# Splits of weight blocks scheduled 64 instructions ahead of their use, between the first gates and the second, in a two-layer hybrid decoder trunk

## The chip, the cores and the metric

The kernel runs on one core of a Trainium2 chip. A core has a matrix engine (TensorE, PE in the profile), a vector engine (VectorE, DVE), a scalar engine (ScalarE, ACT), a general engine (GpSimd, POOL) and a queue engine (SyncE, SP). Each works through its own list of instructions in order and waits for the others by semaphores. The metric is the device time of one execution in microseconds (us).

## The reference

The input is `x`, 512 tokens of width 1024, all in float32. Each of the two layers does this, cut to what matters here:

```python
h = rmsnorm(x, norm_mix)
z = h @ w_in                       # q_a k_a v_a | q_m k_m v_m o_m | i/f logits | gates A, B
att = sliding_window_attention(q_a, k_a, v_a, sinks)  # 8 heads of 64, 2 kv heads, window 128
hm = mlstm_chunkwise(q_m, k_m, v_m, i_pre, f_pre)     # 4 heads, chunks of 64
hm = rmsnorm(hm, m_head_norm) * sigmoid(o_m)
mixed = sigmoid(g_a) * (att @ w_att_branch) + sigmoid(g_m) * (hm @ w_m_branch)
x = x + mixed @ w_out
u = relu(rmsnorm(x, norm_ffn) @ w_ff1)
x = x + (u * u) @ w_ff2            # width 4096
```

## The kernel before

Each layer is a `mixer` (everything up to `mixed @ w_out`) and then an `mlp`. The 512 tokens stay on the chip. Weights come from memory in blocks of 128 rows by 512 columns, and every product is made from float32 numbers that are split in two parts: `wh` is the rounded high part, `wl` the rest. A product of two split numbers is three matmuls (`mm3`).

The function `chunk` (L139) provides one such block. It loads the block into a tile `w` (pool `wraw`, three buffers) by a DMA that SyncE issues (L155), ScalarE copies it to `wh` (L165), and VectorE subtracts `wh` from `w` to get `wl` (L166). The pool `wsp` holds four pairs `wh`, `wl`. So a load needs the split of three blocks before to be done, and a split needs the products of four blocks before to be done. In `group_steps` four result tiles are built over the blocks: a block serves 4 x 3 matmuls, and after the last block `finish` evicts the four results.

The order of the instructions comes from a scheduler. The program is written as one list, and the scheduler takes, of what is ready in its model, the instruction that comes first in priority, which is its place in the program. Code inside `tc.high_priority()` is treated as if it stood in front of everything. With a number, `tc.high_priority(64)`, it is treated as if it stood that many instructions ahead of its own place. `tc.issue_after` adds an edge to the order. All of `chunk` stands in `tc.high_priority()`.

Work of other kinds is put between the matmul steps by `weave(fill, side)`: `fill` is the list of matmul steps with a width, and `side` a list of functions with places along it. In the mixer's first `weave` (it ends at L416) the attention queries, keys and values and the gate logits are projected. In the second, which ends at L1062, the `fill` is the projection of the mLSTM queries and keys, the first half of the branch gates (`s0`, `s1`), the value and output-gate products (`vo_steps`, `a_steps`) and the second half of the gates (`s2`, `s3`); its `side` holds the attention units and the mLSTM's own work.

The pieces of the attention that the prediction names are these. L561 to L564 turn the keys of one block of tokens into `kT`: ScalarE scales the high parts, VectorE subtracts the low part (L563) and casts it (L564) for the second head. L583 and L584 do the same for the queries. The scores are products `aux<-kT,t`; L603 copies them, L610 to L621 are the softmax, L52 transposes the probabilities, L175 and L176 split them, GpSimd masks them by a select (L636), and `aux<-t,v` multiplies them by the values.

The value and output-gate products are made by a scheme of seven products with sums of weight blocks. These sums are built in tiles `a`: SyncE loads one block (L716), GpSimd adds others by accumulating DMAs (L720, L732), and L725 and L726 split the sum. Two of the seven products take plain blocks through `chunk`. L769, L770 and L777 form sums `sc` of the inputs, L680 and L683 are products of the gating, L475 is a scan over the gate logits and L915 multiplies a gate into its result.

Of the kernel before, what the change touches and what calls it, by code (L numbers as in the profile page):

```python
# [33 lines left out]
def hybrid_kernel(ctx, tc, x, norm_mix, w_in, att_q_norm, att_k_norm, att_sinks, m_gate_bias,  # L34
# [27 lines left out]
    def nm(s):  # L62
        uid[0] += 1
        return f"{s}_{uid[0]}"
# [30 lines left out]
    def sm(shape, tag, bufs=None):  # L95
        return small.tile(list(shape), F32, tag=tag, name=nm(tag), bufs=bufs)

    def f32(ap):
        return ap.bitcast(F32)
# [34 lines left out]
        return gcol[:, 32 + 4 * l + k:33 + 4 * l + k]  # L134


    chunks, asked = [0], [None]

    def chunk(src, width=T):  # L139

        with tc.high_priority():
            raw = now["wraw"].tile([P, T], F32, tag="w", name=nm("w"))
            off = 0
            for s in src:
                n = s.shape[1]
                if first_loads:

                    n0 = {0: 0, 1: 2}.get(chunks[0], len(first_loads) - 1)
                    with tc.issue_after(first_loads[n0].ins):
                        first_weights.append(nc.sync.dma_start(raw[:, off:off + n], s))  # L150
                    chunks[0] += 1
                    if chunks[0] == 8:
                        first_loads.clear()
                else:
                    asked[0] = nc.sync.dma_start(raw[:, off:off + n], s)  # L155
                off += n
            wh = now["wsp"].tile([P, T], F32R, tag="wh", name=nm("wh"))
            wl = now["wsp"].tile([P, T], F32R, tag="wl", name=nm("wl"))
            n = chunks[0] - 1 if first_loads else 2
            with ExitStack() as order:  # L160
                if n < 1:

                    order.enter_context(tc.issue_after(norm0.hi[n].ins))
                    order.enter_context(tc.issue_after(norm0.lo[n].ins))
                sc.activation(wh[:, :off], raw[:, :off], AF.Copy)  # L165
                ve.tensor_tensor(wl[:, :off], raw[:, :off], f32(wh[:, :off]), op=ALU.subtract)  # L166
        return wh, wl
# [20 lines left out]
    def group_steps(acts, srcs, evac, width, mm, order=None):  # L188


        order = order or list(range(len(acts)))
        ps, w = [], []

        def step(k, m):
            if k == order[0]:
                ps.append(bank())
            if m == 0:
                w[:] = chunk(srcs(k))
            mm(ps[m], slice(m * P, (m + 1) * P), w, acts[k], k == order[0], k == order[-1])

        def finish():
            with tc.high_priority():
                for m in range(4):
                    evac(m, ps[m][:, :width])

        return [(0.25, lambda k=k, m=m: step(k, m)) for k in order for m in range(4)] + [(0, finish)]

    def feat_steps(acts, srcs, evac):

        def mm(ps, c, w, a, first, last):  # L210
            mm3(ps, w[0][:, c], w[1][:, c], a[0], a[1], first, last)

        return group_steps(acts, srcs, evac, T, mm)
# [8 lines left out]
    def weave(fill, side=()):  # L222

        side = sorted(side, key=lambda e: e[0])
        at = 0.0
        for width, f in fill:
            while side and side[0][0] <= at + 1e-6:
                side.pop(0)[1]()
            f()
            at += width  # L230
        for _, f in side:
            f()
# [155 lines left out]
    def mixer(l, norm, late, order, phase):  # L388
# [9 lines left out]
        def wcols(c0, n):  # L398
            return lambda k: [W[k * P:(k + 1) * P, c0:c0 + n]]
# [16 lines left out]
              late + [(6.9, norm.columns), (11.0, lambda: row.append(norm.along()))])  # L416


        ig = sm([P, NB, MH], "ig", 1)
        fg = sm([P, NB, MH], "fg", 1)  # L420
        fa = sm([P, NB, MH], "fa", 1)
# [390 lines left out]
        def vo_step(n, k, i):  # L812
            which, at, outs = plan[n]
            fresh = n in (5, 1, 2, 4) and k == 0
            if fresh and i == 0:
                held[which] = [bank(), bank()]
            if i == 0:
                ready[k] = weight(n, k)
            wh, wl = ready[k]
            if at:  # L820
                c = slice(H * at[0] + i * P, H * at[0] + (i + 1) * P)
                ah, al = (a[:, c] for a in acts[4 * at[1] + k])
            else:
                ah, al = (a[:, k % 2, i * P:(i + 1) * P] for a in sums[n][k // 2])
            mm3(held[which][i], ah, al, wh, wl, fresh, False, skip_group_check=True)
            if k == 3:
                with tc.high_priority():
                    for f, t, first in outs:
                        f(t, i, held[which][i], first)

        def vo_steps(*ns):
            return [(0.25, lambda n=n, k=k, i=i: vo_step(n, k, i))
                    for n in ns for k, i in (by_tokens if n in (6, 7) else by_weights)]
# [78 lines left out]
        def a_steps(g, sg):  # L912
            def ev_a(m, ps):
                t = sg[m]
                ve.scalar_tensor_tensor(t, t, 1.0, ps, op0=ALU.add, op1=ALU.mult)  # L915

            return feat_steps(att_acts, lambda k: [w_att_branch[l, k * P:(k + 1) * P, 512 * g:512 * g + 512]],
                              ev_a)
# [115 lines left out]
        def ready_w(n, k):  # L1034
# [16 lines left out]
            if n == 3:  # L1051
# [8 lines left out]
        side += [(59.6 + 0.75 * k, lambda k=k: ready_w(1, k)) for k in range(3)]  # L1060
        weave(feat_steps(acts, wcols(C_QM, 512), ev_qk) + s0 + s1 + vo_steps(2) + a_steps(0, g0) + a_steps(1, g1)
              + vo_steps(5, 1, 3, 6, 7, 4) + s2 + s3, side)  # L1062

        def m_step(g, m, k):
            if k == 0:
                now_m[g, m] = bank()
            ps, c = now_m[g, m], slice(m * P, (m + 1) * P)
            mm3(ps, *(w[:, c] for w in wm[g, k]), *hmT[k], k == 0, k == 3)
            if k == 3:
                with tc.high_priority():  # L1070
                    merge(g, m, ps)
                    if m % 2:
                        if g:
                            sum1(m // 2)
                        else:
                            direct(0, 0, m // 2)
# [550 lines left out]
    for l in range(DEPTH):  # L1627
        with start if l == 0 else ExitStack() as phase:
            if l > 0:
                psum_pools(phase, 3)  # L1630
            norm = mixer(l, norm, late, order, phase)
        late = norm.steps(0, 1.5, 0.5)
        with ExitStack() as phase:
            psum_pools(phase, 2)
            norm = mlp(l, norm, late, phase)
        late = norm.steps(0, 1.5, 0.5, lambda k, norm=norm: turn_behind(norm, k)) if norm else []
        order = [4, 5, 6, 7, 0, 1, 2, 3]
# [40 lines left out]
```

## Time and profile before

| | |
|---|---|
| time, median of 3 runs | 1290.96 us (1288.26 to 1292.7) |
| profiled execution | 1292.53 us, span 1290.8 us, granted TensorE clock 1.00 |
| TensorE busy | 1273.2 us, 99% of the span |
| VectorE busy | 1043.5 us, 81% |
| ScalarE busy | 795.5 us, 62% |
| GpSimd busy | 265.0 us, 21% |
| memory read | 188.95 MB, 148 GB/s over the span |

The page is one execution. The span is the time from its first instruction to its last; the execution's own time is a little longer. A row of the timeline has the start in us from the start of the span, the busy time in us, the engine, the line, the operation, the tile written and the tiles read, and the count; in brackets stands the idle time ahead of it and who ended it. Layer 1 repeats layer 0 about 640 us later.

### The profile page before, as it was taken

The numbers are of one execution on the slowest core, as the hardware profiler recorded it, in microseconds if no ns is written. First come the engines' busy times: TensorE is split into PE (matmuls) and PEld (weight loads), VectorE is DVE, ScalarE is ACT, GpSimd is POOL, SyncE is SP. The second block draws the span as 40 slices with busy tenths as digits, with TensorE's granted clock in tenths as the row PEclk, the third lists the DMA queues.
The fourth block names the chain that finished last, engine by engine and source line by source line (L and its number), as shares of the span: only waits on it lengthen the run. The fifth ranks groups of instructions, "written<-read, shape, count | busy, mean of one in ns | idle before, by whom it ended". The sixth has DMA issues, their size and how long they took to land.

```text
span 1290.8 us, 19209 instructions
## 1 busy us (share of the span) xinstructions
PE 1273.2 (99%) x6882; PEld 1086.0 (84%) x6882; DVE 1043.5 (81%) x1650; ACT 795.5 (62%) x1403; POOL 265.0 (21%) x341
## 2 busy tenths in 40 slices
PE   9999999999999999999999999999999999999998
PEld 7877778887889999999888777788788899999987
DVE  4688998678687897969948889886887879879697
ACT  5568568645665666656554775785465656665563
POOL 4502142021003021131114022310310030301210
PEclk9999999999999999999999999999999999999999
DMA  5425372576669888898224253734856697988953
GB/s 156 111 75 155 90 131 74 156 129 141 195 164 182 239 181 210 193 210 214 33 75 115 66 148 92 129 99 135 162 136 195 158 212 195 205 213 192 220 142 98
DMA packets 139503, 194.39 MB, mean 151 GB/s; under 512 B 10632, under 2 KB 79088, under 8 KB 139408
## 3 DMA queue, kind: packets, MB, share of 16 engines
q1 hardware_dynamic: 92992, 129.72, 32.8%
q0 software_dynamic: 45696, 63.05, 30.5%
q8 instruction: 54, 0.88, 0.3%
q10 hardware_dynamic: 720, 0.40, 0.1%
q14 instruction: 41, 0.34, 0.1%
HBM read 188.95 MB, written 2.10 MB: 148 GB/s over the span
## 4 chain that ended last, share of the span: by engine, by line
PE 85%; DVE 7%; DMA 3%; ACT 3%; issue 2%; DVEq 0%; SPq 0%; ACTq 0%
PE mm L47 68%; PE aux L47 16%; PE aux L52 2%; DMA qa<-in_w_out_dram 1%; DMA w<-in_w_in_dram 1%; DVE wl L726 1%; DVE wl L166 1%; DVE p L949 1%; DVE a L948 1%; DVE t L176 1%; ACT wh L165 0%; ACT wh L1159 0%; DVE a L698 0%; DVE p L915 0%; DVE m L610 0%
## 5 line engine op out<-in xcount | busy, mean ns | idle before, releaser
L47 PE MATMUL mm<-i,wh 128*128 128x512 f32 (+1 forms) x1280 | 352.8, 362 | 0.3
L1159 ACT ACTIVATE wh<-raw 128x1024 fp32r<-128x1024 f32 x212 | 223.2, 1056 | 177.0 <-PE mm L47 98.6
L1160 DVE TENSOR_TENSOR wl<-raw,wh 128x1024 fp32r<-128x1024 f32 x212 | 255.6, 1220 | 80.2 <-ACT wh L1159 80.1
L47 PEld LDWEIGHTS mm<-i,wh 128*128 128x128 f32 x1280 | 223.0, 189 | 31.1 <-ACT wh L1159 0.7
L47 PE MATMUL mm<-i,wl 128*128 128x512 f32 (+1 forms) x640 | 229.5, 359 | 0.0
L47 PE MATMUL mm<-wh,uh 128*128 128x512 f32 x440 | 171.8, 390 | 0.0
L47 PE MATMUL mm<-wl,uh 128*128 128x512 f32 x440 | 171.7, 390 | 0.0
L47 PE MATMUL mm<-wh,ul 128*128 128x512 f32 x440 | 171.2, 389 | 0.0
L166 DVE TENSOR_TENSOR wl<-w,wh 128x512 fp32r<-128x512 f32 (+1 forms) x144 | 98.7, 689 | 58.1 <-ACT wh L165 56.4
L1329 POOL DMA_DIRECT2D raw<-in_w_ff_dram x48 | 62.6, 1311 | 382.2 <-DMA raw<-in_w_ff_dram 212.2
L47 PEld LDWEIGHTS mm<-i,wl 128*128 128x128 f32 x640 | 121.0, 189 | 17.7
L165 ACT ACTIVATE wh<-w 128x512 fp32r<-128x512 f32 (+1 forms) x144 | 86.7, 604 | 64.3 <-PE mm L47 38.7
L47 PE MATMUL mm<-wh,i 128*128 128x512 f32 (+1 forms) x352 | 101.0, 360 | 2.9 <-ACT wh L165 2.4
L1214 DVE SCALAR_TENSOR_TENSOR x<-mm,ms,x 128x512 f32<-128x512 f32 x126 | 90.5, 744 | 9.1 <-PE mm L47 8.9
L47 PEld LDWEIGHTS mm<-wh,ul 128*128 128x128 f32 x440 | 82.6, 188 | 17.6
L47 PEld LDWEIGHTS mm<-wh,uh 128*128 128x128 f32 x440 | 82.8, 188 | 16.1
L47 PEld LDWEIGHTS mm<-wl,uh 128*128 128x128 f32 x440 | 82.8, 188 | 15.4
L1486 POOL DMA_DIRECT2D raw<-in_w_ff_dram x36 | 43.2, 1200 | 149.3 <-DVE wl L1160 117.2
L47 PEld LDWEIGHTS mm<-wh,i 128*128 128x128 f32 x352 | 62.0, 188 | 13.8 <-ACT wh L165 3.4
L47 PE MATMUL aux<-i,wh 128*128 128x256 f32 x384 | 69.5, 283 | 0.0
L47 PE MATMUL aux<-t,wh 128*128 128x256 f32 x384 | 69.5, 283 | 0.0
L47 PE MATMUL mm<-wl,i 128*128 128x512 f32 (+1 forms) x176 | 62.1, 353 | 0.5 <-DVE wl L166 0.5
(317 smaller groups left out, 2532.7 us busy)
## 6 DMA issues: line engine op xcount, KB each, us to landing
raw<-in_w_ff_dram SPq DMA_DIRECT2D x144, 512.0 KB, 5.1
raw<-in_w_ff_dram POOLq DMA_DIRECT2D x84, 512.0 KB, 7.8
w<-in_w_in_dram SPq DMA_DIRECT2D x112, 256.0 KB, 2.7
a<-in_w_in_dram POOLq DMA_DIRECT2D x32, 256.0 KB, 5.7
qa<-in_w_out_dram POOLq DMA_DIRECT2D x12, 512.0 KB, 6.0
a<-in_w_in_dram SPq DMA_DIRECT2D x16, 256.0 KB, 5.0
w<-in_w_att_branch_dram SPq DMA_DIRECT2D x16, 256.0 KB, 2.7
w<-in_w_m_branch_dram SPq DMA_DIRECT2D x16, 256.0 KB, 2.9
```

What stands on the lines that cost most here:

```text
L47: latest[0] = nc.tensor.matmul(*args, **kw)
L52: latest[0] = nc.tensor.transpose(*args)
L165: sc.activation(wh[:, :off], raw[:, :off], AF.Copy)
L166: ve.tensor_tensor(wl[:, :off], raw[:, :off], f32(wh[:, :off]), op=ALU.subtract)
L176: last_split[1] = ve.tensor_tensor(lo, src, f32(h), op=ALU.subtract)
L726: ve.tensor_tensor(wl, r, f32(wh), op=ALU.subtract)
L948: ve.scalar_tensor_tensor(sgm[g][m], sgm[g][m], 1.0, ps, op0=ALU.add, op1=ALU.mult)
L1159: sc.activation(hi, src, AF.Copy)
L1160: ve.tensor_tensor(lo, src, f32(hi), op=ALU.subtract)
L1214: ve.scalar_tensor_tensor(xh[:, cc], ps[i][:, cc], ms[j][:, b:b + 1], xh[:, cc], op0=ALU.mult, op1=ALU.add)
L1329: gp.dma_start(to[h], src(h, i, j), accum_op=ALU.add)
L1486: gp.dma_start(to[h], src(h, i, j), accum_op=ALU.add)
```

## The change

The split of a block in `chunk` is taken out of the first `tc.high_priority()` and put into a second one, whose argument is `lead[0]`. `None` is the default: in front of everything, as before. In each layer `lead[0]` is 64 from the end of the first `weave` to the end of the second. The load of the block stays as it was.

```diff
-    chunks, asked = [0], [None]
+    chunks, asked, lead = [0], [None], [None]
...
                 else:
                     asked[0] = nc.sync.dma_start(raw[:, off:off + n], s)
                 off += n
+        with tc.high_priority(lead[0]):
             wh = now["wsp"].tile([P, T], F32R, tag="wh", name=nm("wh"))
             wl = now["wsp"].tile([P, T], F32R, tag="wl", name=nm("wl"))
...
               late + [(6.9, norm.columns), (11.0, lambda: row.append(norm.along()))])
 
+        lead[0] = 64
         ig = sm([P, NB, MH], "ig", 1)
...
         weave(feat_steps(acts, wcols(C_QM, 512), ev_qk) + s0 + s1 + vo_steps(2) + a_steps(0, g0) + a_steps(1, g1)
               + vo_steps(5, 1, 3, 6, 7, 4) + s2 + s3, side)
+        lead[0] = None
```

Behind the first added line, the kernel's lines move by 1, behind the second by 2 and behind the third by 3. No engine has an instruction more or less.

**The attention, on VectorE.** Around the cast that completes `kT` for the last block of tokens in layer 0 (`wl_314`, `wl_324`, `wl_335` and `wl_343` are the splits of four consecutive blocks). Before:

```order
L564 CAST kT_110_623<-kT_110_623 64x128
L166 TENSOR_TENSOR wl_335_1615<-w_333_1612,wh_334_1614 128x512
L584 SCALAR_TENSOR_TENSOR t_255_1258<-aux_253_1248,gc0_137,t_255_1258 64x256 x2
L619 TENSOR_TENSOR den_259_1278<-den_259_1278,es_258_1276 128x4
L620 RECIPROCAL den_259_1278<-den_259_1278 128x4
L621 TENSOR_TENSOR t_240_1197<-t_240_1197,den_259_1278 128x512
L166 TENSOR_TENSOR wl_343_1646<-w_341_1643,wh_342_1645 128x512
L563 SCALAR_TENSOR_TENSOR kT_110_623<-aux_263_1296,gc1_147,kT_110_623 64x128
L603 COPY_PREDICATED t_264_1306<-tri_l_79,aux_265_1307 128x256
L564 CAST kT_110_623<-kT_110_623 64x128
L176 TENSOR_TENSOR t_268_1323<-aux_266_1317,t_267_1322 128x512
```

After:

```order
L586 SCALAR_TENSOR_TENSOR t_255_1258<-aux_253_1248,gc0_137,t_255_1258 64x256 x2
L621 TENSOR_TENSOR den_259_1278<-den_259_1278,es_258_1276 128x4
L565 SCALAR_TENSOR_TENSOR kT_110_623<-aux_263_1296,gc1_147,kT_110_623 64x128
L622 RECIPROCAL den_259_1278<-den_259_1278 128x4
L605 COPY_PREDICATED t_264_1306<-tri_l_79,aux_265_1307 128x256
L623 TENSOR_TENSOR t_240_1197<-t_240_1197,den_259_1278 128x512
L566 CAST kT_110_623<-kT_110_623 64x128
L167 TENSOR_TENSOR wl_314_1517<-w_312_1514,wh_313_1516 128x512
L177 TENSOR_TENSOR t_268_1323<-aux_266_1317,t_267_1322 128x512
L605 COPY_PREDICATED t_264_1306<-tri_l_79,aux_279_1372 128x256
L167 TENSOR_TENSOR wl_324_1570<-w_322_1567,wh_323_1569 128x512
```

Before, all four splits stand ahead of the last `CAST kT`, two of them in these rows. After, all four stand behind it, the first two in these rows.

**The attention, on TensorE.** `aux_266` are transposes of probabilities, `aux_271` products with the values, `aux_279` and `aux_286` scores against the `kT` above; the `mm` rows with `wh_299` and with `wh_313` are two blocks of 12 matmuls that follow each other. Before:

```order
L52 MATMUL aux_266_1317<-ident_71,t_222_1114 128x128 x4
L47 MATMUL mm_274_1358<-i_5_114,wl_314_1517 128x512
L47 MATMUL mm_278_1368<-i_5_114,wh_313_1516 128x512
L47 MATMUL mm_278_1368<-i_6_115,wh_313_1516 128x512
L47 MATMUL mm_278_1368<-i_5_114,wl_314_1517 128x512
L47 MATMUL mm_283_1393<-i_5_114,wh_313_1516 128x512
L47 MATMUL mm_283_1393<-i_6_115,wh_313_1516 128x512
L47 MATMUL aux_271_1336<-t_243_1210,v2_111_625 128x512
L47 MATMUL aux_271_1336<-t_244_1211,v2_111_625 128x512
L47 MATMUL aux_271_1336<-t_245_1214,v2_111_625 128x512
L47 MATMUL aux_271_1336<-t_246_1215,v2_111_625 128x512
L47 MATMUL aux_279_1372<-kT_110_623,t_216_1072 128x256 x4
```

After:

```order
L47 MATMUL mm_284_1397<-i_5_114,wl_289_1412 128x512
L47 MATMUL mm_274_1358<-i_5_114,wh_299_1456 128x512
L52 MATMUL aux_266_1317<-ident_71,t_222_1114 128x128 x4
L47 MATMUL aux_271_1336<-t_243_1210,v2_111_625 128x512
L47 MATMUL aux_271_1336<-t_244_1211,v2_111_625 128x512
L47 MATMUL aux_271_1336<-t_245_1214,v2_111_625 128x512
L47 MATMUL aux_271_1336<-t_246_1215,v2_111_625 128x512
L47 MATMUL aux_279_1372<-kT_110_623,t_216_1072 128x256 x4
L47 MATMUL mm_274_1358<-i_6_115,wh_299_1456 128x512
L47 MATMUL mm_274_1358<-i_5_114,wl_300_1457 128x512
```

Before, all of this stands inside the block `wh_313`, `aux_279` behind its ninth row. After, it stands behind the first matmul of the block before, `wh_299`.

**The loads, on SyncE.** `w` are plain blocks, `a` the tiles of the sums. Before:

```order
L155 DMA w_322_1567<-in_w_in_dram 128x512
L155 DMA w_333_1612<-in_w_in_dram 128x512
L155 DMA w_341_1643<-in_w_in_dram 128x512
L155 DMA w_347_1675<-in_w_in_dram 128x512
L716 DMA a_358_1729<-in_w_in_dram 128x512
L716 DMA a_362_1744<-in_w_in_dram 128x512
L716 DMA a_367_1779<-in_w_in_dram 128x512
L155 DMA w_352_1703<-in_w_in_dram 128x512
L716 DMA a_373_1798<-in_w_in_dram 128x512
L716 DMA a_390_1854<-in_w_in_dram 128x512
L716 DMA a_394_1868<-in_w_in_dram 128x512
L155 DMA w_359_1732<-in_w_in_dram 128x512
```

After:

```order
L155 DMA w_322_1567<-in_w_in_dram 128x512
L155 DMA w_333_1612<-in_w_in_dram 128x512
L718 DMA a_358_1729<-in_w_in_dram 128x512
L718 DMA a_362_1744<-in_w_in_dram 128x512
L718 DMA a_367_1779<-in_w_in_dram 128x512
L718 DMA a_373_1798<-in_w_in_dram 128x512
L718 DMA a_390_1854<-in_w_in_dram 128x512
L718 DMA a_394_1868<-in_w_in_dram 128x512
L718 DMA a_395_1876<-in_w_in_dram 128x512
L155 DMA w_341_1643<-in_w_in_dram 128x512
L155 DMA w_347_1675<-in_w_in_dram 128x512
L155 DMA w_352_1703<-in_w_in_dram 128x512
```

Before, `w_341` and `w_347` stand ahead of all `a` loads, and `w_352` and `w_359` among them. After, seven `a` loads stand ahead of `w_341`.

**The value blocks, on VectorE.** `wl_443`, `wl_446`, `wl_451` and `wl_454` are the splits of plain blocks, `wl_436` and `wl_461` those of sums. Before:

```order
L726 TENSOR_TENSOR wl_436_2061<-a_373_1798,wh_435_2060 128x512
L475 SCALAR_TENSOR_TENSOR t_405_1916<-aux_406_1917,mp_97_589,neg_82 4x128
L769 SCALAR_TENSOR_TENSOR sc_382_1824<-sc_382_1824,i_33_277 128x1024
L166 TENSOR_TENSOR wl_443_2082<-w_441_2079,wh_442_2081 128x512
L166 TENSOR_TENSOR wl_446_2094<-w_444_2091,wh_445_2093 128x512
L770 TENSOR_TENSOR sc_382_1824<-sc_382_1824,i_34_278 128x1024
L166 TENSOR_TENSOR wl_451_2112<-w_449_2109,wh_450_2111 128x512
L494 TENSOR_TENSOR cm2_100_595<-t_405_1916,cm2_100_595 4x512
L176 TENSOR_TENSOR t_423_1999<-sc_382_1824,t_422_1998 128x512
L498 TENSOR_TENSOR em_98_590<-aux_434_2053,bl_93_585 128x16
L166 TENSOR_TENSOR wl_454_2124<-w_452_2121,wh_453_2123 128x512
L726 TENSOR_TENSOR wl_461_2149<-a_390_1854,wh_460_2148 128x512
```

After:

```order
L167 TENSOR_TENSOR wl_443_2082<-w_441_2079,wh_442_2081 128x512
L477 SCALAR_TENSOR_TENSOR t_405_1916<-aux_406_1917,mp_97_589,neg_82 4x128
L177 TENSOR_TENSOR t_423_1999<-sc_382_1824,t_422_1998 128x512
L167 TENSOR_TENSOR wl_446_2094<-w_444_2091,wh_445_2093 128x512
L177 TENSOR_TENSOR t_425_2003<-sc_382_1824,t_424_2002 128x512
L167 TENSOR_TENSOR wl_451_2112<-w_449_2109,wh_450_2111 128x512
L496 TENSOR_TENSOR cm2_100_595<-t_405_1916,cm2_100_595 4x512
L500 TENSOR_TENSOR em_98_590<-aux_434_2053,bl_93_585 128x16
L682 TENSOR_TENSOR a_448_2106<-a_171_868,a_447_2103 64x512
L685 TENSOR_TENSOR a_455_2135<-a_173_872,a_455_2135 64x512
L167 TENSOR_TENSOR wl_454_2124<-w_452_2121,wh_453_2123 128x512
L728 TENSOR_TENSOR wl_461_2149<-a_390_1854,wh_460_2148 128x512
```

Ahead of `wl_443` now stand both `sc` operations of the sum `sc_382` (L772 was L770), and the scan (L477, was L475) and the product `a_448` (L682, was L680) went behind it. The `sc` operation of L777 (now L779), which stood behind `wl_454`, is now also far ahead of these rows, and `t_425` and `a_455` have come ahead of `wl_454`.

## The prediction

> **What bounds the kernel now.** I read the page's totals first, then busy time by stretch, then the timelines of the two places where TensorE waits.
>
> ```profile
> span 1290.8 us, 19209 instructions
> PE 1273.2 (99%) x6882; PEld 1086.0 (84%) x6882; DVE 1043.5 (81%) x1650; ACT 795.5 (62%) x1403; POOL 265.0 (21%) x341
> 60.00:100.00 40.00, 38.83 (x200) 31.30 (x199) 33.31 (x77) 27.97 (x83) 7.50 (x21) 1.00 0.26 72
> 100.00:142.00 42.00, 41.19 (x196) 31.96 (x195) 37.05 (x89) 33.10 (x92) 10.36 (x15) 1.00 0.55 148
> 142.00:160.00 18.00, 18.00 (x89) 14.63 (x89) 17.20 (x39) 7.91 (x17) 1.48 (x1) 1.00 0.34 95
> 160.00:191.00 31.00, 29.61 (x128) 22.92 (x127) 28.10 (x49) 22.30 (x43) 16.63 (x18) 1.00 0.72 124
> 700.00:740.00 40.00, 38.85 (x198) 31.18 (x197) 33.34 (x78) 28.48 (x84) 6.99 (x20) 1.00 0.26 68
> 740.00:782.00 42.00, 40.47 (x193) 31.35 (x192) 37.44 (x88) 32.61 (x91) 9.97 (x15) 1.00 0.55 145
> 800.00:831.00 31.00, 29.70 (x129) 23.15 (x128) 28.22 (x47) 22.11 (x43) 17.03 (x18) 1.00 0.70 124
> ```
>
> TensorE is busy for 99% of the span, so a split costs time only where TensorE waits for it, or where it makes something else late. The lower rows are the stretches that the change reorders, in both layers: from and to, length, then the busy time and count of TensorE (PE), its weight loads, VectorE, ScalarE and GpSimd, the granted clock, the DMA share and GB/s. TensorE idles there for 1.17 + 0.81 + 0 + 1.39 = 3.37 us in layer 0 and 1.15 + 1.53 + 1.30 = 3.98 us in layer 1. These **7.35 us** are all that shorter waits could give back. VectorE has 6.7 + 4.95 = 11.6 us free between 60 and 142, and almost none from 142 to 160 (17.20 of 18).
>
> **First place: the attention of the last units, around 110.** Here is what VectorE, TensorE and GpSimd do there before; the last two rows are layer 1.
>
> ```profile
> 103.27 0.68 DVE L166 TENSOR_TENSOR wl<-w,wh 128x512 fp32r<-128x512 f32 x1
> 113.75 0.23 DVE L564 CAST kT<-kT 64x128 fp32r<-64x128 f32 x1
> 107.66 0.61 PE L47 MATMUL mm<-i,wh 128*128 128x512 f32 x2
> 110.38 0.61 PE L47 MATMUL mm<-i,wh 128*128 128x512 f32 x2
> 111.17 0.66 PE L52 MATMUL aux<-ident,t 128*128 128x128 f32 x4 [0.18 <-DVE t L584]
> 113.39 1.17 PE L47 MATMUL aux<-t,v 128*128 128x512 f32 x4 [0.18 <-DVE kT L563]
> 114.39 1.12 PE L47 MATMUL aux<-kT,t 128*128 128x256 f32 x8
> 120.38 0.75 PE L47 MATMUL aux<-kT,t 128*128 128x256 f32 x4 [0.44 <-DVE t L176]
> 115.64 0.86 POOL L732 DMA_DIRECT2D a<-in_w_in_dram  x1 [2.17 <-DMA a<-in_w_in_dram]
> 117.89 0.89 POOL L636 TENSOR_SCALAR_AFFINE_SELECT t<-t 128x512 fp32r<-128x512 f32 x1 [0.16 <-ACT t L175]
> 757.48 1.08 PE L47 MATMUL aux<-t,v 128*128 128x512 f32 x2 [0.45 <-POOL t L636]
> 760.79 0.74 PE L47 MATMUL aux<-kT,t 128*128 128x256 f32 x4 [0.58 <-DVE t L176]
> ```
>
> Before, four splits stand on VectorE in the 11 us ahead of the cast that completes `kT`, which ends at 113.98; the row quoted is the first. After, all four stand behind it. The cast therefore ends at about 113.98 - 4 x 0.68 = 111.3. But TensorE's order moves further than VectorE's time. The score product `aux_279`, which needs that cast, started at 114.39. It now stands behind the first matmul of block `wh_299`, which starts at 107.66: plus 0.2 for this matmul, 0.4 for four transposes (0.66 long, the last overlapped) and 1.0 for the four products `aux_271` (113.39 to 114.39 before), it is reached at 109.3.
>
> That is a new wait of 111.3 - 109.3 = **2.0 us**. Its bounds: ScalarE too has four copies fewer ahead of its last part of `kT`, some 0.6 each; if 1.5 of these 2.4 us add to VectorE's, 0.5 is left. If only 1.7 of VectorE's 2.7 come through, as the scores that it normalises in between set the pace, it is 3.0. I take 2.0, since the last steps are VectorE's. Queued behind the waiting product are all other matmuls of block `wh_299`, and VectorE's eviction of them.
>
> Against this, the small waits go: 0.18 + 0.18 + 0.44 = 0.8 in layer 0, and 0.45 + 0.58 = 1.0 in layer 1. The SyncE loads of the `a` tiles now stand ahead of three `w` loads, so GpSimd's accumulate no longer waits 2.17 us for one and no longer holds the select behind it.
>
> One table load stands ahead of this chain, before and after.
>
> ```profile
> 100.31 1.28 ACT L701 ACT_TABLE_LOAD   x1
> 101.60 0.63 ACT L701 ACTIVATE p<-p 128x512 f32<-128x512 f32 x1
> ```
>
> The next activation starts 0.01 us after it, so I charge 1.28 us, the same on both sides. The Trainium skill ("ScalarE: Activation LUTs", What ACT_TABLE_LOAD costs) counts a drain of 1.38 us on top for every switch; by it the cast would come 1.4 later, and the total below would be about 1.6 us higher. The trace shows no such drain here.
>
> **The splits themselves.** Before, the one at 103.27 (`wl_314`) is ready 7 us ahead of its block at 110.38. After, it stands right behind the cast and ends at about 112.0, while some 4 us of attention (0.4 + 1.0 + 1.0, and 0.4 + 1.0 of the next unit) have moved ahead of the block, which starts after 114. I charge 0. The moved loads have a price of the same kind:
>
> ```profile
> 113.25 0.45 SPq L716 DMA_DIRECT2D a<-in_w_in_dram  x1
> DMA to landing us min/median/max: 2.7/5.3/5.9
> ```
>
> `w_341` now stands behind the last `a` load. This went out at 113.25 before, so `w_341` lands by 113.6 + 5.9 = 119.5 and is split by 121. Its block comes four blocks of 2.72 (107.66 to 110.38) and those 4 us later than 107.66, at 122.5 or after. That cover is 1.5 us; without it, TensorE would pay the difference. I charge 0.
>
> **Second place: the value blocks, around 176.** TensorE's largest wait in layer 0 stands here, and VectorE, the load and TensorE form one chain.
>
> ```profile
> 160.53 0.65 DVE L680 TENSOR_TENSOR a<-a,a 64x512 fp32r<-64x512 f32 x1
> 167.80 0.47 DVE L475 TENSOR_TENSOR_SCAN t<-aux,mp,neg 4x128 f32<-4x128 f32 x1
> 169.31 1.27 DVE L166 TENSOR_TENSOR wl<-w,wh 128x512 fp32r<-128x512 f32 x2
> 170.51 1.21 DVE L770 TENSOR_TENSOR sc<-sc,i 128x1024 f32<-128x1024 f32 x1
> 176.55 0.69 DVE L166 TENSOR_TENSOR wl<-w,wh 128x512 fp32r<-128x512 f32 x1 [2.71 <-ACT wh L165]
> 177.76 0.68 DVE L176 TENSOR_TENSOR t<-sc,t 128x512 fp32r<-128x512 f32 x1
> 179.08 0.69 DVE L683 TENSOR_TENSOR a<-a,a 64x512 fp32r<-64x512 f32 x1
> 182.21 1.22 DVE L777 TENSOR_TENSOR sc<-sc,i 128x1024 f32<-128x1024 f32 x1
> 170.01 7.59 SPq L155 DMA_DIRECT2D w<-in_w_in_dram  x4
> 175.89 0.63 ACT L165 ACTIVATE wh<-w 128x512 fp32r<-128x512 f32 x1 [2.93 <-DMA w<-in_w_in_dram]
> 176.57 0.50 PE L47 MATMUL mm<-wh,i 128*128 128x512 f32 x1 [0.94 <-ACT wh L165]
> 177.30 0.50 PE L47 MATMUL mm<-wl,i 128*128 128x512 f32 x1 [0.23 <-DVE wl L166]
> ```
>
> The load of `w_452` goes out at 170.01, as the split `wl_443` (first of the two at 169.31) frees its buffer; it lands at 175.9, and TensorE waits 0.94 + 0.23 = **1.17 us**. After, ahead of `wl_443` stand the two long `sc` operations (1.22 + 1.21), while an `a` product (0.65) and a scan (0.47) went behind it: **+1.3 us** on the load. Ahead of `wl_454` stand 1.22 + 0.68 + 0.69 = 2.6 us more than before in all, which fit into the 2.71 us that VectorE idles before it; beyond the later load they cost nothing, unless VectorE is later by more than that.
>
> Against the 1.3 stands idle time of VectorE in the attention stretch that is refilled, since it no longer waits there for `wh`. It is between 0 and the 4.95 us free there; I take 0.7, one split, because new waits for ScalarE take the place of most.
>
> **The sum.** Per layer, TensorE reaches the value blocks 2.0 - 0.8 = 1.2 us later (1.0 in layer 1). The load is 1.3 - 0.7 = 0.6 later. The old 1.17 us of wait absorbs TensorE's delay (1.2 - 1.17 = 0.03), so the later of the two ends sets it: +0.6 per layer, +1.2 in all. The profiled execution took 1292.53 us, 1.7 above its span and 1.6 above the median of 1290.96; I put the difference on the median: 1290.96 + 1.2 = **1292.2**. Its own range: 0 or 1.4 refilled in each layer moves this by 1.4 either way, and a first wait of 3.0 puts TensorE's end (1.0) behind the load's (0.6): with both, some 1290 to 1295.
>
> **Rivals.**
> *Faster.* `kT` comes without delay and VectorE reaches the value blocks early. One more wait then shrinks:
>
> ```profile
> 85.61 0.74 PE L47 MATMUL aux<-kT,t 128*128 128x256 f32 x4 [0.73 <-DVE t L603]
> ```
>
> Here one split (0.68) leaves VectorE's path, though the product is also asked for 0.45 earlier. With 0.7 here, 0.8 at 110 and 0.9 of the 1.17 at 176, each layer gains 2.4, so 1290.96 - 4.8 = 1286.2; all idle time back would be 1283.6. For it: VectorE's 11.6 free microseconds. Against: attention products move ahead on TensorE by as much as their inputs do.
>
> *Slower: the chain on VectorE becomes the bound.* TensorE's delay of 1.2 in the attention stretch passes through the evictions into a VectorE that has no slack from 142 on, and the 1.3 comes on top: 2.5, or 3.5 with the first wait at its upper end; I take 3.0 in each layer, so 1297. It decides once VectorE starts `wl_443` after 171.3 (169.31 + 2.0). For it: 17.20 of 18 busy. Against: TensorE's delay also gives VectorE time.
>
> *Slower by the clock.* A longer stall could lower TensorE's granted clock, and every matmul would take twice as long at half.
>
> ```profile
> 250.00:300.00 50.00, 47.79 (x216) 38.58 (x215) 36.83 (x56) 23.23 (x37) 12.01 (x12) 1.00 0.71 148
> PE mm L47 <- ACT a L175: 2.2, 1, 2.2
> ```
>
> A wait of 2.2 us passed at a granted clock of 1.00, and mine is expected at 2.0, up to 3.0. A few microseconds at half clock would cost some 2 in each layer: 1296. The Trainium skill ("TensorE: Matmul & The Clock Gate", HAM oscillation) puts the fall at idle gaps over about 3.4 us, which neither bound here reaches; no run shows one.
>
> That the change does nothing is out: the order of all engines shows the splits moved.
>
> **The numbers.** Forecast 0.40 (0.36 of it within the band, 0.04 above), faster 0.27 (0.24 beyond, 0.03 within), VectorE's chain 0.28 (0.26 beyond, 0.02 within), clock 0.05. A measurement here can tell about 0.3%, or 3.9 us, from no change. So faster 0.24, same 0.41, slower 0.35. The range goes from the faster case's far end, 1284, to 1300, where the slower one has 3.5 in each layer and 2 for the clock.
>
> **What would show it.** Right: a wait of about 2 us at `aux<-kT,t` near 109 to 112, the load of `w_452` about 0.6 us later with a wait of the old size behind it, GpSimd's select without the wait ahead of it, clock 1.00. Wrong on the first step: no wait at `kT`. Wrong on the second: `wl_443` earlier than 169.3, or later than 171.3; then the rivals hold. A clock under 1.00 in either stretch would speak for the third. A wait at block `wh_342` would show that moving the loads was not free.

## The result, and the profile after

| | before | after |
|---|---|---|
| median, us | 1290.29 (1288.26 to 1293.0, 7 runs) | 1284.52 (1283.18 to 1284.89, 7 runs) |
| profiled execution, us | 1292.53, span 1290.8 | 1284.8, span 1283.1 |

The ratio of after to before is 0.9948, with a 95% interval of 0.9936 to 0.9960. The forecast was 0.1% slower; the change is 0.5% faster. Run twice more beside the kernel before, it gave 0.9954 (0.9934 to 0.9974) and 0.9967 (0.9955 to 0.9978).

The page's totals of the changed kernel, the group of the splits on VectorE, and the two stretches around the value blocks (from and to, length, busy time and count of TensorE, weight loads, VectorE, ScalarE, GpSimd, then granted clock, DMA share, GB/s):

```profile
span 1283.1 us, 19225 instructions
PE 1267.5 (99%) x6882; PEld 1088.1 (85%) x6882; DVE 1038.5 (81%) x1650; ACT 795.6 (62%) x1403; POOL 260.6 (20%) x341
L167 DVE TENSOR_TENSOR wl<-w,wh 128x512 fp32r<-128x512 f32 (+1 forms) x144 | 97.4, 678 | 46.2 <-ACT wh L166 45.1
160.00:191.00 31.00, 31.00 (x140) 25.41 (x139) 28.45 (x51) 21.96 (x43) 12.74 (x17) 1.00 0.79 134
800.00:831.00 31.00, 31.00 (x143) 25.46 (x142) 27.65 (x52) 23.75 (x50) 10.96 (x16) 1.00 0.69 123
```

In both layers TensorE now has no idle time in the value stretch (before: 1.39 and 1.30 us). Over the whole program VectorE waits 46.2 us ahead of these splits; the same group of before has this row:

```profile
L166 DVE TENSOR_TENSOR wl<-w,wh 128x512 fp32r<-128x512 f32 (+1 forms) x144 | 98.7, 689 | 58.1 <-ACT wh L165 56.4
```

**The first place, around 110.** TensorE and VectorE in the timeline of after:

```profile
111.13 0.64 PE L47 MATMUL aux<-kT,t 128*128 128x256 f32 x4
111.25 0.22 DVE L566 CAST kT<-kT 64x128 fp32r<-64x128 f32 x1
112.85 0.74 PE L47 MATMUL aux<-kT,t 128*128 128x256 f32 x4
114.95 1.16 PE L47 MATMUL aux<-t,v 128*128 128x512 f32 x4 [0.23 <-DVE t L653]
```

The cast comes at 111.25, almost where the forecast had it. But the product `aux_279` starts at 111.13, ahead of it: it does not need it. The next scores, `aux_286`, which do, start 1.4 us after the cast's end. There is no wait of 2 us.

**The second place, around 175.** VectorE, SyncE and ScalarE in the timeline of after, and how long the loads around it take to land:

```profile
168.34 0.67 DVE L167 TENSOR_TENSOR wl<-w,wh 128x512 fp32r<-128x512 f32 x1
169.04 6.92 SPq L155 DMA_DIRECT2D w<-in_w_in_dram  x4
174.25 0.63 ACT L166 ACTIVATE wh<-w 128x512 fp32r<-128x512 f32 x1 [1.52 <-DMA w<-in_w_in_dram]
174.91 0.69 DVE L167 TENSOR_TENSOR wl<-w,wh 128x512 fp32r<-128x512 f32 x1 [0.91 <-ACT wh L166]
DMA to landing us min/median/max: 2.7/3.9/5.1
```

`wl_443` is at 168.34 instead of 169.31, so the load of `w_452` goes out 1.0 us earlier, and it lands faster too (5.1 at most, against 5.9). Its copy is at 174.25 instead of 175.89, and TensorE does not wait.

**Where the time went, by TensorE's place.** Windows of the same times compare different work, as the traces shift against each other. So each matmul of a trace was assigned to its row in TensorE's order, and matmuls that stand at the same place in both orders were compared. The table gives how much less (-) or more (+) a trace takes than the first profile of before between such places: the first attention (71.71 to 146.78 in before) and value stretch (to 191.53), those of layer 1 (690.06 to 787.18, to 833.58), and all else. All numbers are us.

| trace | attention 0 | value 0 | attention 1 | value 1 | all else | sum |
|---|---|---|---|---|---|---|
| before, second profile | -1.02 | -1.25 | -0.55 | +0.82 | +1.41 | -0.59 |
| after | -0.89 | -2.62 | -2.00 | -2.54 | +0.35 | -7.70 |
| after, second | -0.86 | -2.62 | -2.01 | -2.53 | +0.21 | -7.81 |
| after, third | -0.85 | -2.62 | -2.00 | -2.54 | +2.96 | -5.05 |
| lead outside value blocks | -0.64 | -2.28 | -1.77 | -2.25 | +0.84 | -6.10 |
| lead on value blocks only | -1.37 | -2.51 | -1.27 | -2.05 | -0.24 | -7.44 |
| after, `a` loads behind | -0.85 | -2.62 | -1.98 | -2.53 | -1.96 | -9.94 |
| late `wl` | +0.10 | -2.62 | -0.21 | -2.54 | +3.44 | -1.83 |
| late `wh` | -1.01 | -0.70 | -2.17 | -0.23 | +5.20 | +1.09 |
| before, 4 buffers | -1.05 | -2.17 | -1.92 | -2.08 | +4.36 | -2.86 |
| after, 4 buffers | -0.88 | -2.62 | -2.01 | -2.53 | +2.80 | -5.24 |
| before, 4 buffers in layer 1 | -1.06 | -1.55 | -1.91 | -2.08 | +1.50 | -5.10 |
| after, late load | -0.83 | -1.76 | -1.98 | -1.29 | -0.26 | -6.12 |
| lead 128 | +0.24 | -2.32 | -1.12 | -2.24 | +0.84 | -4.60 |
| lead 32, first | -0.92 | -2.60 | -1.75 | -0.72 | +0.18 | -5.81 |
| lead 32, second | -0.92 | -2.53 | -1.69 | -2.51 | +3.82 | -3.83 |
| lead 16 | -0.87 | -2.62 | -1.69 | -2.51 | +2.54 | -5.15 |

Three profiles of after agree within 0.05 us in all four stretches. The two of before differ by up to 1.3 us in a stretch: there TensorE waits, directly or behind another engine, for a load, and how long it waits hangs on how fast the load lands. Against the mean of the two, after gains 2.0 and 2.9 us in the value stretches, and 0.4 and 1.7 in the attention. TensorE's idle time tells only a part of this: in the four stretches it falls from 7.4 us in the first profile of before to 4.0 in after, while the stretches lose 8.05 us. A matmul beside a wait takes longer (0.50 us at 176.57 in before, 0.39 to 0.40 in a row without waits) and counts as busy.

The part outside, with the first loads of the program, moves by some us from one profile to the next with the same code (after: +0.21 to +2.96), so one profile says nothing of a microsecond there. Some of this is the granted clock. It stayed at 1.00 in both profiles of before and the first two of after. In the third of after it fell to 0.50 for 3.41 us, right behind a wait of TensorE; first the wait, then the windows around the fall:

```profile
928.60 1.68 PE L47 MATMUL mm<-i,a 128*128 128x512 f32 x6 [2.21 <-ACT a L176]
926.00:930.10 4.10, 1.90 (x9) 1.24 (x8) 3.34 (x5) 0.63 (x1) 2.14 (x2) 1.00 0.71 162
930.10:933.51 3.41, 3.41 (x10) 2.63 (x9) 1.12 (x2) 1.81 (x4) 0.86 (x1) 0.50 0.90 157
933.51:937.00 3.49, 3.49 (x17) 2.86 (x16) 2.93 (x4) 1.57 (x4) 2.20 (x3) 1.00 0.87 150
```

The same stands once in "after, 4 buffers" and twice in "late `wl`", "late `wh`", "before, 4 buffers" and "lead 32, second": ten falls, apart from the program's last two microseconds, each within 1.6 us behind the end of a wait of 1.8 to 2.5 us, and all outside the four stretches. By an estimate from the 3.41 us at half clock each costs 1.7 us. Waits of 2.2 to 2.4 us also passed without a fall (both profiles of before near 295), so the wait alone does not decide it.

### The profile page after: what moved, and what is told of

The parts are those of the page before. It is cut to its first block, busy times and chain, and to the rows that moved or that the text cites. A ratio compares the mean times of both kernels' runs of the same rounds, so it can differ in the third digit from the quotient of the medians.

```text
span 1283.1 us, 19225 instructions
## 1 busy us (share of the span) xinstructions
PE 1267.5 (99%) x6882; PEld 1088.1 (85%) x6882; DVE 1038.5 (81%) x1650; ACT 795.6 (62%) x1403; POOL 260.6 (20%) x341
## 4 chain that ended last, share of the span: by engine, by line
PE 86%; DVE 5%; ACT 5%; DMA 2%; issue 1%; DVEq 0%; SPq 0%; ACTq 0%
PE mm L47 70%; PE aux L47 15%; PE aux L52 2%; DMA qa<-in_w_out_dram 1%; ACT t L618 1%; DVE wl L167 1%; DVE p L951 1%; DVE a L950 1%; DMA w<-in_w_in_dram 1%; ACT wh L1162 0%; ACT wh L166 0%; DVE t L653 0%; DVE a L700 0%; ACT t L585 0%; ACT p L703 0%
## 5 line engine op out<-in xcount | busy, mean ns | idle before, releaser
L167 DVE TENSOR_TENSOR wl<-w,wh 128x512 fp32r<-128x512 f32 (+1 forms) x144 | 97.4, 678 | 46.2 <-ACT wh L166 45.1
```

## The experiments

Theory A: splits in front of everything stand in VectorE's queue waiting for `wh`, and all work behind them waits too; placed later, they leave VectorE ahead of time at the value blocks, where the load of `w_452` hangs on it. Theory B: the splits of the value blocks themselves got a better place. Theory C: the `a` loads, now ahead on SyncE, bring the gain.

**The change in two parts.** `e1_not_value` gives the lead to all but the plain value blocks, `e2_only_value` to these alone.

```diff
 def weight(n, k):
     if n in (1, 2):
-        return chunk([block(n - 1, 0, k)])
+        keep, lead[0] = lead[0], None      # e1; e2: lead[0] = 64 here, None elsewhere
+        w = chunk([block(n - 1, 0, k)])
+        lead[0] = keep
+        return w
```

> The lead of 64 for all blocks of the second weave but the plain blocks of the value products (those two products keep their splits in front of everything). Theory A, VectorE's queue: the splits of the query, key and gate blocks no longer stand in front of VectorE's other work waiting for their wh, so VectorE comes to the value blocks earlier; nearly all of the gain of 5.8 us stays, 1284 to 1286. Theory B, the value blocks' own splits sit better: little of the gain stays, 1288.5 to 1290.5. Of the ledger of the two traces (3.1 us in the attention stretches, 5.1 in the value stretches, 1.1 behind them) theory B would lose the 5.1.

> The counterpart: the lead of 64 for the plain blocks of the value products alone. Theory A: no gain, 1289 to 1291. Theory B: 1284.5 to 1287.

Measured: 0.9976 (0.9966 to 0.9986) and 0.9977 (0.9965 to 0.9989). Neither theory has it as it was put: by the ratios each part has about half of the time. In the traces, each of the two alone takes most of the waits out of both value stretches, and its four stretches together lose nearly what those of after lose (-6.9 and -7.2, against -8.05). Why the time then shows only half is not shown. So what the value stretches need is VectorE somewhat earlier, from whichever splits; theory A's "nearly all with e1" fell, and so did B's "none with e1".

**The loads.** `e3_a_behind` is the changed kernel with the `a` loads behind `w_347` (`log` lists the loads that `chunk` issues in the second `weave`; the edge goes to the 24th).

```diff
 def load(r, i, j, k):
-    nc.sync.dma_start(r, block(i, j, k))
+    with tc.issue_after(log[23].ins):
+        nc.sync.dma_start(r, block(i, j, k))
```

> The changed kernel with one thing put back: the loads of the a tiles stand behind the loads of w_341 and w_347 on SyncE again, as before; TensorE's order is that of the changed kernel. Theory C, the loads: the accumulates on GpSimd come late again and hold the selects behind them, so 2 us or more of the gain go, 1286.5 to 1290. Theories A and B: within 1 us of the changed kernel, 1283.5 to 1285.5.

Measured: 0.9966 (0.9954 to 0.9979), 1283.82 us. SyncE and GpSimd in layer 1 of this kernel:

```profile
747.79 1.85 SPq L721 DMA_DIRECT2D a<-in_w_in_dram  x4
751.35 3.55 POOL L737 DMA_DIRECT2D a<-in_w_in_dram  x4
```

The `a` loads go out at 747.8, no earlier than before (746.07 there), and the accumulates start at 751, and still all four stretches are as in after. So the `a` loads need not be early, and theory C falls as it was put. But GpSimd's order changed with them: the first selects now stand ahead of the accumulates, so no select is held by a late one. That half of theory C is not tested here; the fourth buffer in layer 1, below, bears on it.

**Which half of a split.** `e7_wl_late` schedules only VectorE's subtraction 64 ahead, `e8_wh_late` only ScalarE's copy.

```diff
-        with tc.high_priority(lead[0]):
+        with tc.high_priority():           # e8: lead[0]
...
                 sc.activation(wh[:, :off], raw[:, :off], AF.Copy)
+        with tc.high_priority(lead[0]):    # e8: no argument
...                                         # the edge for the first block, as above
                 ve.tensor_tensor(wl[:, :off], raw[:, :off], f32(wh[:, :off]), op=ALU.subtract)
```

> Of the split only VectorE's subtraction is scheduled 64 ahead; ScalarE's copy to wh stays in front of everything. Theory A (VectorE's queue is freed): most of the gain stays, 0.995 to 0.997 of before. If instead it is ScalarE that was blocked by the copies, little stays, 0.998 to 1.000.

> The counterpart: ScalarE's copy is scheduled 64 ahead, VectorE's subtraction in front of everything. In the order the subtraction follows its copy at once, so VectorE is asked for it as soon as the copy is done. Theory A: less of the gain than with the late subtraction, 0.997 to 1.000. If ScalarE was the blocked one: 0.995 to 0.997.

Measured: 0.9972 (0.9961 to 0.9983) and 0.9992 (0.9980 to 1.0003). The second lies within theory A's range; the first is 0.0002 outside of it and nearer to it than to the other. First the load on SyncE with the late `wl`, then the load and TensorE's and VectorE's waits with the late `wh`:

```profile
168.74 5.48 SPq L155 DMA_DIRECT2D w<-in_w_in_dram  x4
```

```profile
170.52 7.20 SPq L155 DMA_DIRECT2D w<-in_w_in_dram  x4
176.67 0.69 DVE L171 TENSOR_TENSOR wl<-w,wh 128x512 fp32r<-128x512 f32 x1 [2.32 <-ACT wh L166]
176.69 0.50 PE L47 MATMUL mm<-wh,i 128*128 128x512 f32 x1 [0.97 <-ACT wh L166]
```

With VectorE's half late, the load goes out at 168.7 and the value stretches are as in after. With ScalarE's half late, it goes out at 170.5 and the wait of 0.97 is back. But the attention of layer 1 is the other way round: -2.17 with the late copy, -0.21 with the late subtraction. In these two kernels the value stretches go with VectorE's half and the attention of layer 1 with ScalarE's (in layer 0 the -1.01 is no more than the second profile of before has). The order of the loads moved with the halves. SyncE in layer 1, late `wh`, then late `wl`:

```profile
740.45 2.79 SPq L722 DMA_DIRECT2D a<-in_w_in_dram  x6
748.62 2.00 SPq L722 DMA_DIRECT2D a<-in_w_in_dram  x4
```

With the late copy six `a` loads go out in one row; with the late subtraction the last four stand behind `w` loads, and GpSimd's accumulates are late, as in before.

**The load of `w_452` itself.** Four buffers let it go out one split earlier (`e9_raw4` on before, `e10_raw4_after` on after).

```diff
-    pool(phase, "wraw", 3)
+    pool(phase, "wraw", 4)
...
-    pool(phase, "act", 23)
+    pool(phase, "act", 22)
```

> The kernel before with four buffers for the loaded blocks instead of three (and 22 instead of 23 tiles in the pool of the a tiles, for the room). The load of w_452 then needs the split of a block one earlier, and goes out before wl_443 is done. If the chain wl_443 to load to split to TensorE is what the change shortens in the value stretches (theory A), its wait goes in both layers without touching the splits' places: about 2.0 to 3.5 us, 0.997 to 0.9985 of before. If the gain of the value stretches has another source, nothing: 0.999 to 1.001.

> The changed kernel with the same four buffers. No wait for w_452 is left to remove, so theory A expects no further gain: 0.995 to 0.996 of before, as the changed kernel. If loads are late elsewhere too, it is below 0.9945.

Measured: 1.0003 (0.9989 to 1.0016) and 0.9983 (0.9969 to 0.9996): no gain, where theory A had 0.997 to 0.9985; and on after a smaller gain than the 0.995 to 0.996 of theory A. The traces tell why the times can't decide. TensorE at the start of e9, then of e10:

```profile
12.73 0.50 PE L47 MATMUL mm<-wh,i 128*128 128x512 f32 x1 [2.49 <-ACT i L178]
```

```profile
12.68 0.50 PE L47 MATMUL mm<-wh,i 128*128 128x512 f32 x1 [2.78 <-ACT i L179]
```

With a fourth buffer SyncE puts one more weight load ahead of the loads of `x`, and TensorE waits 2.5 to 2.8 us for its first input (0.47 in before). In e9 the clock falls behind this wait:

```profile
13.50:16.91 3.41, 3.37 (x10) 2.80 (x11) 1.44 (x2) 1.32 (x2) 0.84 (x4) 0.50 0.92 216
```

Over all runs, 7 of the 12 of e9 and 9 of the 12 of e10 had a mean clock of 0.998 or less, against 4 of the 35 of before beside them. The two runs of e9 at 1.00 average 1286.5 us, the 22 of before at 1.00 1288.7; two runs are few, but so taken the gain is what theory A had. In the value stretches the waits are gone (-2.17, -2.08). So the fourth buffer was then given to layer 1 alone.

```diff
-    pool(phase, "wraw", 3)
+    pool(phase, "wraw", 4 if l else 3)
...
-    pool(phase, "act", 23)
+    pool(phase, "act", 22 if l else 23)
```

> The kernel before with four buffers for loaded blocks (and 22 tiles in the pool of the a tiles) in layer 1 alone. Theory A: TensorE's wait at the value blocks of layer 1 goes, 2.1 us against the profile of before as with four buffers in both layers, and the start is as before: 0.998 to 0.9992 of before. In the trace: layer 0 as before, layer 1 without a wait near 817. If the load of w_452 is not the cause: the waits on TensorE in the value stretch stay.

Measured: 0.9990 (0.9980 to 1.0001). SyncE in layer 1 of this kernel, and at the same place in before:

```profile
805.91 5.68 SPq L155 DMA_DIRECT2D w<-in_w_in_dram  x4
```

```profile
810.39 7.48 SPq L155 DMA_DIRECT2D w<-in_w_in_dram  x4
```

The loads go out 4.5 us earlier, 3.4 of which this trace is ahead there anyway. The value stretch of layer 1 is 2.08 us shorter with the splits where they were, and the time lies within what theory A gave, though its interval just holds no change.

The attention of layer 1 is 1.91 us shorter too, which no theory had. TensorE's order there is that of before, so single rows can be compared: 1.0 us is gained at the product at 757.48 and 0.9 at the scores at 760.79, the two waits that the prediction quotes. GpSimd and VectorE just ahead of them, in before and then in this kernel:

```profile
755.91 0.86 POOL L732 DMA_DIRECT2D a<-in_w_in_dram  x1 [3.18 <-DMA a<-in_w_in_dram]
756.46 2.12 POOL L636 TENSOR_SCALAR_AFFINE_SELECT t<-t 128x512 fp32r<-128x512 f32 x3
756.36 2.78 DVE L166 TENSOR_TENSOR wl<-w,wh 128x512 fp32r<-128x512 f32 x1
```

```profile
752.75 0.86 POOL L732 DMA_DIRECT2D a<-in_w_in_dram  x1 [1.60 <-DMA a<-in_w_in_dram]
753.30 1.54 POOL L636 TENSOR_SCALAR_AFFINE_SELECT t<-t 128x512 fp32r<-128x512 f32 x2
754.96 0.69 DVE L166 TENSOR_TENSOR wl<-w,wh 128x512 fp32r<-128x512 f32 x1
```

In before the last accumulate waits 3.18 us for an `a` load, three selects are held behind it, and the split beside these selects takes 2.78 us instead of 0.69. With the fourth buffer this accumulate comes 1.8 us earlier by TensorE's place, and the split keeps its 0.69. The late `wl`, which gains little here, has such a split too (2.51 us), and the second profile of before as well (2.25). Where the selects are not held in this way (after, the late `wh`, the `a` loads behind), no split in the attention takes over 1.2 us. So in the attention, too, the wait seems to hang on a load. This is read from the traces and not shown by a run of its own: other splits beside a select took 0.7 us, and what sets a long one apart is open.

`e14_reuse` does the opposite on after: the last plain block is loaded into the tile of the block ahead of it.

```diff
-            raw = now["wraw"].tile([P, T], F32, tag="w", name=nm("w"))
+            raw = hold[1] if hold[0] else now["wraw"].tile([P, T], F32, tag="w", name=nm("w"))
+            hold[1] = raw                  # hold[0] is set for n == 1 and k == 3
```

> The changed kernel, but the last plain value block is loaded into the tile of the block just ahead of it, so that its load must wait for wl_451 instead of wl_443, some 2.8 us later. Theory A: TensorE's wait comes back, 1.5 to 2.5 us in each layer, and 3 to 5 us of the gain are lost: 0.9975 to 0.9995 of before. If the load is not the cause, the gain stays: 0.995 to 0.996.

Measured: 0.9968 (0.9957 to 0.9980), the same as after beside it (0.9967). ScalarE and TensorE in layer 0, then TensorE in layer 1:

```profile
175.36 0.63 ACT L167 ACTIVATE wh<-w 128x512 fp32r<-128x512 f32 x1 [2.39 <-DMA w<-in_w_in_dram]
176.04 0.73 PE L47 MATMUL mm<-wh,i 128*128 128x512 f32 x2 [0.48 <-ACT wh L167]
812.09 0.74 PE L47 MATMUL mm<-wh,i 128*128 128x512 f32 x2 [0.86 <-ACT wh L167]
```

The wait returns, but with 0.48 and 0.86 it is a third of what I expected, as the copy comes only 1.1 us later than in after (1.6 by TensorE's place, as this trace is 0.5 ahead). The table shows 0.86 and 1.25 us lost in the value stretches; the time does not resolve this. The trace supports the chain, the time is inconclusive.

**How far ahead.** Only the number is changed.

```diff
-        lead[0] = 64
+        lead[0] = 128                      # e11 and e16: 32; e12: 16
```

> A lead of 128 instructions instead of 64. Theory A: the splits move back towards the front of VectorE's queue, and part of the gain is lost: 1285 to 1288. If what counts is only that the splits are not in front of everything, it is the same as with 64, 1284 to 1285.

> A lead of 32 instructions; TensorE's order is that of the changed kernel. Theory A: VectorE's queue is as free as with 64 and the splits still come in time: 0.994 to 0.9965. If 64 is close to the edge at which splits come late, TensorE waits at blocks and part of the gain is lost: 0.997 or more.

> A lead of 16; TensorE's order is again that of the changed kernel. Here I expect splits to come late: waits for wl or wh at the starts of blocks, some 0.2 to 0.5 us each at 10 to 20 blocks, 0.997 to 1.002 of before. Without such waits, as with 64.

> The lead of 32 beside the lead of 64. In the two traces both have the same waits up to 800 us; behind that 32 has 2 us more at w_452 of layer 1. I expect it between: 0.996 to 0.998 where 64 has 0.995. Equal ratios would say that the difference of e11 to the changed kernel was the chip's.

Measured: 0.9982 (0.9970 to 0.9993) for 128, 0.9994 (0.9982 to 1.0007) and 0.9983 (0.9973 to 0.9993) for 32, 0.9984 (0.9970 to 0.9997) for 16. The loss of gain with 128 is as theory A has it, and shows in the attention (+0.24 and -1.12). Theory A's range for 32 (0.994 to 0.9965) was missed both times. Only one session has 32 beside 64 (0.9983 and 0.9967), and 16 was run without 64 beside it. That 32 and 16 are worse by 0.15% or more is not explained: TensorE's order is the same, and in three of the four stretches, or all, their traces are within about 0.3 us of that of 64. It is not the clock alone: in the session with both, the runs at 1.00 average 1286.3 us with 32 (5 runs) and 1283.9 with 64 (2 runs). The waits for splits that I expected with 16 don't appear.

**Both kernels again.**

> The kernel before, unchanged, for a second profile of it. In all five profiles with a lead the load of w_452 goes out earlier and TensorE's wait of 0.94 + 0.23 us for it is gone, yet the times differ. If the wait belongs to the kernel before (theory D, a fixed chain), it stands in this profile too, in both layers, with the load near 170 and 810 less the start. If it was chance in the one profile (theory E, how long a load takes to land), it is absent or smaller here, and the difference of the two spans must be told without it. The time must be that of the kernel before, within 0.1%.

> The changed kernel, unchanged, on the same chip as its neighbours. The ratio of 0.9948 should come again, within 0.15%; if the first chip was kind to it, 0.996 to 0.998 as for the kernels with half of the change.

> The changed kernel beside its neighbours: 0.995 to 0.996 of before, as on two occasions. If it comes out at 0.998 here, chips differ in what the change is worth.

Measured: 1.0002 (0.9989 to 1.0015), 0.9954 and 0.9967 (intervals above). The load and TensorE's waits in the second profile of before:

```profile
170.13 6.35 SPq L155 DMA_DIRECT2D w<-in_w_in_dram  x4
176.18 0.50 PE L47 MATMUL mm<-wl,i 128*128 128x512 f32 x1 [0.19 <-DVE wl L166]
816.92 0.50 PE L47 MATMUL mm<-wh,i 128*128 128x512 f32 x1 [1.64 <-ACT wh L165]
817.65 0.50 PE L47 MATMUL mm<-wl,i 128*128 128x512 f32 x1 [0.22 <-DVE wl L166]
```

The load goes out at the same place, and the wait is 0.19 in layer 0 and 1.86 in layer 1. So both theory D and E hold in part: the chain is fixed, its wait is drawn anew by the landing of the load each time. Before stands on the edge; after stands off it.

## Why the prediction was wrong

**The new wait at `kT` (2.0 us in each layer): wrong.** This was the first term, and its step was that `aux_279` "needs that cast". It reads `t_216`, queries of the third block of tokens, and the parts of `kT` up to that block, which were cast long before; the cast at 111.25 is for the fourth block. `kT` is one tile with one name, and I took the last writer in the list for the one that is waited for. What the runs show in place of the 2.0 us is no wait at all for the cast. Before, both products ran as one group of 8 at 114.39, behind the cast, and that hid it. The cast's time (111.3 forecast, 111.25 measured) came out that close by luck: by TensorE's places, the trace of after stands 1.3 us later than before at the start of this stretch and 0.4 at its end. TensorE came to `aux_279` at 111.13, not at 109.3, so even a real need for the cast would have cost some 0.3 us.

**The later load of `w_452` (+0.6 us): wrong in sign.** This is the step on which the forecast turned, as the sum took the later of its two ends, and this was it. The price of the rows moved ahead of `wl_443`, +1.3, was right: just those rows moved. The term that was mis-sized is the refill, 0.7. VectorE up to `wl_443`, before and after, and the group of its splits of 128x512 in that time, before and after:

```profile
0.00:169.31 169.31, 164.89 (x826) 133.36 (x826) 130.90 (x299) 107.27 (x268) 56.20 (x103) 1.00 0.43 115
L166 DVE TENSOR_TENSOR wl<-w,wh 128x512 fp32r<-128x512 f32 x45 | 32.2, 715 | 15.8 <-ACT wh L165 15.4
```

```profile
0.00:168.34 168.34, 162.52 (x820) 133.03 (x821) 130.24 (x299) 107.37 (x267) 53.17 (x103) 1.00 0.44 116
L167 DVE TENSOR_TENSOR wl<-w,wh 128x512 fp32r<-128x512 f32 x45 | 32.1, 715 | 12.3 <-ACT wh L166 12.0
```

The waits ahead of splits fell by 3.5 us, of which 1.6 are left as less idle time in all (38.41 to 38.10, with 1.33 us of later start to take off). And the busy time did not rise by 1.31 but fell by 0.66: about 1.0 us more of it is overlap of operations that follow each other without a gap, and about 1.0 is operations that took less time. So the refill was 1.6 + 2.0 = 3.6 us instead of 0.7, and `wl_443` came 2.3 us earlier against the start, not 0.6 later. I had bounded the idle time (4.95 free) rightly and chosen far too low in it, and had no term for overlap.

**The wait of 1.17 us as the size of the second place: too small.** Placed by TensorE's rows, the value stretch of layer 0 loses 2.62 us against after: 1.7 at `w_452` (the waits, and slow matmuls around them that count as busy) and 0.9 at later splits of `a`. And it was one draw: the second profile has other waits at the same place.

**The rivals.** The faster one was right in its mechanism and close in size (1286.2 forecast, 1284.5 measured): VectorE reaches the value blocks early and the waits shrink, though it put 0.7 on a wait at 85.61 which stayed. The 7.35 us of idle time, from which its far end was taken, was no bound: the stretches lost more than that, since a wait also costs busy time. "VectorE's chain becomes the bound" fell with the wait that was to feed it. The clock stayed at 1.00 in the profile of after, and the gain is there at an equal clock: the runs at 1.00 average 1289.3 us before (18) and 1284.1 after (5) in one session, 1288.3 (14) and 1283.9 (2) in another. But the clock rival's mechanism exists here: the falls above came behind waits of 1.8 to 2.5 us, shorter than the gap that the prediction named for it. What I charged at 0 stayed at 0: TensorE has no wait above 0.2 us for a split in the attention, the block `wh_342` included. For this block that was in part luck: the landing of at most 5.9 us that I used is of the loads at 166 to 178, and among those at 104 to 118 one took 7.6. The sentence against the faster rival, that products move ahead as much as their inputs, held for layer 0 (0.4 us gained) but not for layer 1 (1.7).

**The table load.** ScalarE in after:

```profile
101.77 1.28 ACT L703 ACT_TABLE_LOAD   x1
103.06 2.19 ACT L703 ACTIVATE p<-p 128x512 f32<-128x512 f32 x4
```

The next activation starts 0.01 us behind the load, as before. The drain of 1.38 us that the Trainium skill counts for every switch ("ScalarE: Activation LUTs", What ACT_TABLE_LOAD costs) shows in neither trace.

**What stays open.** In the profiles, the four stretches give after 7 us over the mean of before, and the medians 3 to 6. Both profiles of before are slow ones among their runs (1292.5 and 1291.9 us, with medians of 1290.3 and 1290.2), which may be some 2 us of this; the rest is in the part outside them, which one profile can't resolve. So the causes above are those of the waits in the traces, and how much of the time each is worth is not shown. Why a lead of 64 is faster than 32 and 16 is not settled.

## What to carry to other kernels

A preparation step scheduled in front of everything occupies its engine's queue from the moment it is placed there, done or waiting, and here the cost came out far downstream, where a load waits for that engine to free a buffer; look for the chain from a full engine through a buffer to a load. When a step is said to wait for a tile, follow which part of it is read, not the tile's name. And where TensorE's wait hangs on a load's landing, one profile is one draw: take a second before a term is built on it.

## What was not expected of the hardware

The same load of 256 KB at the same place took up to 5.9 us to land in one profile of before and up to 5.1 in after, and the wait behind it was 0.19 to 1.86 us in profiles of one kernel. VectorE, with the same number of operations and 1.3 us more work in them, was busy for 0.66 us less, partly because operations without gaps between them overlap. A split that takes 0.69 us took 2.78 beside three selects on GpSimd. And the granted clock fell to 0.50 for 3.41 us behind waits of 1.8 to 2.5 us in some executions, while waits of the same size passed without a fall in others.
